# Three edits to a two-layer attention and recurrence kernel: a norm moved ahead, one pair of products reordered, and a duration changed in the table that orders the work

## The chip, the cores and the metric

The kernel runs on one core of a Trainium2 chip. The metric is the device time of one execution in microseconds (us). Five engines take part: PE (matrix products, with PEld for its weight loads), DVE (vector operations), ACT (activations, copies, casts), POOL (little used here) and SP (which issues the DMAs). Each engine works through its own list of instructions strictly in order and waits on semaphores for the others. All times below come from the profile of one execution of the kernel before, and from its three timed runs.

## The reference

The input is one sequence of 1024 tokens with 1024 features, everything in float32.

- Layer 0: RMS norm, then attention with a sliding window of 128 keys and a learned sink per head (16 query heads, 4 key and value heads of 64, rotary embedding on 16 of the 64 dimensions), an output projection, and the residual sum. Then RMS norm and an MLP `square(relu(h @ w_up)) @ w_down` with 4096 hidden units, and the residual sum.
- Layer 1: RMS norm, then a gated linear recurrence (HGRN2) with 8 heads of 128 by 128 state, in chunks of 64 tokens: `o_intra` needs, for each pair of tokens t >= s of a chunk, `sum_d q[t,d] * exp(b[t,d] - b[s,d]) * k[s,d]`, where `b` is the running sum of the log forget gates; `o_inter` comes from the state. Then a norm, an output gate, a projection and the residual sum. Then the same MLP.
- A final RMS norm.

## The kernel before, in words

**Tiling.** Activations stand transposed: 8 tiles of 128 features by 512 tokens for each half (hf 0 and 1) of the tokens. A product in full precision is made of three passes (`mm3`): each operand is split into a high and a low part, and high by high, high by low and low by high are summed in PSUM. Each pass is one matmul of 128x512. The MLPs and the projections of layer 1 use Strassen-like products: seven products named 1 to 7 in place of eight.

**What sets the order.** Python code first records every operation with its operands (`Schedule.add`), the engines that may do it, and a cost in nanoseconds for each. `Schedule.order` then plays the program through with these costs, engine by engine: whenever an engine is free in this play it takes the ready operation with the best rank. PE operations are ranked by their place in the program, the others by a due time worked back from PE, and `lead` moves an operation's rank ahead by 120 ns for each unit. Buffers of a kind (58 `a`, 20 `t`, 7 `m`, 4 `p` and 4 `q` PSUM banks and so on) are given out in the order of the program, as earlier ones come free in the play. What comes out is one sequence of all operations, which is issued in just that order, and the semaphores are put in by the framework from it: where an instruction stands later in the sequence than another that reads or writes the same buffer, it waits for that one. The costs are therefore not on the chip; they only decide the order.

**The norm of layer 0's second half.** `attention` projects half 0 (`qkv(0)`), loads half 1 of x, scales it by the gain (`scaled`), and then interleaves `attend(0)` with `qkv(1)`, and `attend(1)` with `o_proj(0)`. The norm itself is one number per token, `token_rstd(sum_squares(...))`: eight squares on ACT, seven sums on DVE, four narrow matmuls into a PSUM bank of kind `q`, then a chain of six small operations on DVE with a square root on ACT between the first and the second. It is applied when a projection leaves PSUM. `scaled` returns it as a function, and `qkv(1)` calls that at its first step, which comes after the first piece of `attend(0)`.

**The MLP's first products.** `pair(m)` (m = 0 to 15) works out hidden tiles m and m+16 by the seven products; 1, 6, 7 and 4 add up in one bank, `main`, and are read out between (u1, u2, u3, and at the end relu and square); 5 and 3 add up in `side`, 2 has a bank `own`. Each product is 12 matmuls. Behind the last pair, `down` starts: it needs the four `q` banks as its own `main` and the four `p` banks as `side`.

**The recurrence.** For each of the 8 heads (e) the score matrix of a chunk is built in six levels (lg 0 to 5): `products` makes a batch of 16 narrow matmuls (8 for each half, in alternating halves of the PE columns, so 64x32 outputs, or 64x64 for the diagonal), and `merge` on DVE copies the wanted elements into `scores` under a mask. Levels 1 and 2 share one PSUM bank, and so do levels 3 and 4: 16 matmuls of `first` go to `low`, 16 of `second` to `high`, then `merge(low)` and `merge(high)`. Before each level `double` updates q and k on DVE, and `copied` makes copies on ACT. Between the batches PE works on the projections of later heads (`two`), and at the end on `hgrn_out`. The line of `products` that the change touches gives PE's cost of each narrow matmul: `mm` turns its rate into `n * rate / 2.4 + 3` nanoseconds, so 30 for a 64x32 and 58 for a 64x64.

Nearly all rows of the profile name line 372, where every operation is issued, so tiles and shapes tell them apart: `q<-t,t 128*64 128x32` is a narrow product (each is recorded as two matmuls), `q<-a,wh 128*128 128x512` a pass of a wide one, DVE's `COPY_PREDICATED t<-c,q` a merge.

Of the kernel before, what the change touches and what calls it, by code (L numbers as in the profile page):

```python
# [25 lines left out]
MT = FF // P  # L26
# [9 lines left out]
BPH = NBLK // NH  # L36
# [6 lines left out]
CH = 64  # L43
# [93 lines left out]
LEAD = 100  # L137
# [181 lines left out]
class Net:  # L319
# [323 lines left out]
    def pair(self, m, x):  # L643

        w = self.strassen_weights(*(self.io["up"][self.layer, i] for i in (m, m + MT // 2)))

        def read(ps):
            z = self.t()
            self.take(z, ps)
            return z  # L650

        main, side, own = self.psum("q"), self.psum("q"), self.psum()
        self.product(main, w[1], x[1], True)
        u1 = read(main)
        self.product(own, w[2], x[2], True)
        self.product(side, w[5], x[5], True)
        p5 = read(side)
        self.product(main, w[6], x[6], False)
        u2 = read(main)
        self.product(side, w[3], x[3], False)  # L660
        self.product(main, w[7], x[7], False)
        u3 = read(main)
        self.product(main, w[4], x[4], False)
        def kept(name, z):
            self.hid[name, m] = self.keep(z)

        self.add_bank(u1, own)
        h00 = self.square_relu(u1)
        kept(1, h00)
        self.add_bank(u2, side)  # L670
        h01, t5, t6, t4 = self.square_relu(u2), *(self.t() for _ in range(3))
        self.tt("any", t5, h01, h00, ALU.subtract)
        kept(5, t5)
        self.tt("any", p5, p5, u3, ALU.add)
        h11 = self.square_relu(p5)
        kept(3, h11)
        self.tt("any", t6, h11, t5, ALU.subtract)
        kept(6, t6)
        self.tt("any", h01, h11, h01, ALU.subtract)
        kept(7, h01)  # L680
        h10 = self.square_relu(main, True)
        kept(2, h10)
        self.tt("any", t4, h10, t6, ALU.subtract)
        kept(4, t4)
# [374 lines left out]
    def attention(self, layer):  # L1059
        self.v, self.dv, self.ks, self.kl = [], [], [None] * 3, [None] * 3  # L1060
        self.q = [[None] * 2 for _ in range(NBLK)]
        out = [{}, {}]
        self.load_x([0])
        h = [self.scaled(layer, 0)]
        self.attention_constants()
        run(self.qkv(0, *h[0]))
        self.load_x([1])
        h.append(self.scaled(layer, 1))
        interleave(self.attend(0, out[0]), self.qkv(1, *h[1]), 16, 24)
        interleave(self.attend(1, out[1]), self.o_proj(0, out[0]), 24, 8)  # L1070
        self.mlp_first(layer)
        run(self.o_proj(1, out[1]))
# [172 lines left out]
    def recurrence(self, e, ready, totals, out):  # L1245
# [3 lines left out]
        chunk = lambda z, j: z[:, j * CH : j * CH + CH]  # L1249
# [7 lines left out]
        def moved(lg):  # L1257
            return [(k, [parts(chunk(q, j), lg)[:, :, 1] for j in range(2 * BPH)]) for q, f, k, g in gates]
# [10 lines left out]
        def products(part, operands, late, width=CH // 2):  # L1269
            part = part.rearrange("p (c t) -> p c t", c=NC)  # L1270
            for hf, (k, qs) in enumerate(operands):
                for c in range(BPH):
                    for b in range(2):
                        rows = slice(b * CH, b * CH + CH)
                        j = 2 * c + b
                        self.mm(part[rows, hf * BPH + c], chunk(k, j), qs[j], True, True, width, 2.06, "columns", late)

        def merge(part, lg):
            H = 1 << lg
# [6 lines left out]
        def views(operands):  # L1286
            return [z for k, qs in operands for z in (k, *qs)]
# [8 lines left out]
        gates = decayed  # L1296
        late = views(plain) + views(moved(0))
        products(whole, plain, late, CH)
        products(half, moved(0), late)
        mask = self.diag.unsqueeze(1).to_broadcast([P, NC, CH])  # L1300
        self.tt("DVE", scores, whole.rearrange("p (c t) -> p c t", c=NC), mask, ALU.mult)
        merge(half, 0)
        yield
        for lg in range(1, LEVELS, 2):
# [5 lines left out]
            if lg < LEVELS - 1:  # L1310
                second = moved(lg + 1)
                late = views(first) + views(second)
                products(low, first, late)
                products(high, second, late)
                merge(low, lg)
                merge(high, lg + 1)
            else:
                late = views(first) + [z for q, f, k, g in gates for z in (q, k)]
                products(low, first, late)
                cross = self.psum("q")[:CH].rearrange("p (c t) -> p c t", c=NC)  # L1320
                for hf, (q, f, k, g) in enumerate(gates):
                    for c in range(BPH):
                        self.mm(cross[:, hf * BPH + c], chunk(k, 2 * c), chunk(q, 2 * c + 1), True, True, CH, 3.9, "columns", late)
                merge(low, lg)
                weights = []
                for hf in range(NH):
                    s, c = self.t(F32, (P, BPH, 2, CH)), slice(hf * BPH, hf * BPH + BPH)
                    self.memset(s[CH:, :, 0].only(0), 0.0, "Pool")
                    self.copy(s[:CH, :, 0].only(1), scores[:CH, c], 4 * CH)
                    self.copy(s[CH:, :, 1].only(2), scores[CH:, c], 4 * CH)  # L1330
                    self.copy(s[:CH, :, 1].only(3), cross[:, c], 4 * CH)
                    weights.append(s)
                at, tot = self.double(CH, gates, tot, tots, at)
# [149 lines left out]
def run(pieces):  # L1483
    for _ in pieces:
        pass


def interleave(main, other, n_main, n_other):
    done = 0
    for k, _ in enumerate(main):  # L1490
        while done * n_main < (k + 1) * n_other and next(other, run) is not run:
            done += 1
    run(other)
# [81 lines left out]
```

## Time and profile before

| what | value |
|---|---|
| median of 3 runs | 2010.9 us (2010.59 to 2011.6) |
| the profiled execution | 2007.87 us, its span 2005.5 us |
| PE busy | 1979.5 us, 99% of the span, granted clock 0.998 |
| DVE, ACT, POOL busy | 1699.2, 1013.7, 62.7 us |
| chain that ended last | PE 85%, DVE 7%, DMA 3%, issue 2%, ACT 2% |
| 64x32 narrow products | 1536 records (768 products), 51.0 us busy |
| layer 1's recurrence | about 1010 to 1335 us from the span's start |

The span runs from the first to the last instruction; the profiled execution's own time is 2.4 us longer, and 3.0 us below the median of the runs. PE is busy almost throughout, so a list of the places where PE waits says more here than the shares of busy time: `idle before` in a group's row, or a number in square brackets behind a row of the timeline, is PE's idle time ahead of that instruction, and the arrow names what ended it. In the timeline the first column is the start from the beginning of the span, the second the duration of the merged rows; matmuls are pipelined, so the starts that follow each other tell what one costs.

### The profile page before, as it was taken

Reading aid. Unit: us, or ns where it says so; the run is one execution under the profiler, and the core shown is the slowest. Engines: PE = TensorE matmul, PEld = TensorE weight load, DVE = VectorE, ACT = ScalarE, POOL = GpSimd, SP = SyncE. Lnnn points to the kernel's source line nnn. Section 1 sums busy time; section 2 is a strip of 40 time slices with the busy share of each in tenths; the row PEclk is TensorE's granted clock in tenths of the full one; section 3 lists DMA queues with packets and bytes.
Section 4 is the critical chain, followed back from the end, with each engine's and each line's share of the span. In section 5 each row is a group of like instructions: output and inputs, shape, how many; then the busy total and the mean of one; then the engine's idle time right before and its main releaser. Section 6 shows DMA issues by size and latency. Waiting matters only on the chain.

```text
span 2005.5 us, 32701 instructions
## 1 busy us (share of the span) xinstructions
PE 1979.5 (99%) x11404; PEld 1718.5 (86%) x11404; DVE 1699.2 (85%) x3360; ACT 1013.7 (51%) x2045; POOL 62.7 (3%) x124
## 2 busy tenths in 40 slices
PE   9999999999999999999999999999999999999998
PEld 8877788888888888888888888888888888888887
DVE  8999899777778878799898999989977777887787
ACT  6567796554454323255345555554654445323352
POOL 4030100000000000000000000000000000000001
PEclk9999999999999999999999999999999999999999
DMA  6212463544468967745422212667444446886752
GB/s 216 90 53 59 127 222 120 184 167 160 146 204 292 314 217 264 235 163 176 146 63 78 78 59 90 207 208 244 142 167 160 146 162 237 286 301 215 236 179 85
DMA packets 196677, 345.88 MB, mean 172 GB/s; under 512 B 21536, under 2 KB 31776, under 8 KB 196512
## 3 DMA queue, kind: packets, MB, share of 16 engines
q1 hardware_dynamic: 195936, 343.28, 52.0%
q8 instruction: 89, 1.46, 0.3%
q14 instruction: 76, 0.62, 0.1%
q10 hardware_dynamic: 576, 0.52, 0.1%
HBM read 250.39 MB, written 93.32 MB: 171 GB/s over the span
## 4 chain that ended last, share of the span: by engine, by line
PE 85%; DVE 7%; DMA 3%; issue 2%; ACT 2%; POOL 0%; SPq 0%; POOLq 0%; DVEq 0%; ACTq 0%
PE q L372 51%; PE p L372 34%; DVE t L372 3%; DVE a L372 2%; DVE wl L372 1%; ACT t L372 1%; ACT a L372 1%; DMA wr<-in_down 1%; DVE m L372 0%; DMA a<-in_x 0%; ACT wh L372 0%; ACT m L372 0%; DMA t<-d 0%; DMA wr<-in_wqkv 0%; DMA wr<-in_wv 0%
## 5 line engine op out<-in xcount | busy, mean ns | idle before, releaser
L372 PE MATMUL q<-a,wh 128*128 128x512 f32 x2560 | 761.8, 379 | 3.5 <-ACT t L372 3.5
L372 PE MATMUL p<-a,wh 128*128 128x512 f32 x2112 | 644.6, 383 | 0.1
L372 PEld LDWEIGHTS q<-a,wh 128*128 128x128 f32 x2560 | 482.3, 189 | 74.1 <-ACT t L372 5.0
L372 PE MATMUL q<-a,wl 128*128 128x512 f32 x1280 | 484.9, 379 | 0.0
L372 PEld LDWEIGHTS p<-a,wh 128*128 128x128 f32 x2112 | 394.2, 189 | 54.6 <-issue 1.2
L372 PE MATMUL p<-a,wl 128*128 128x512 f32 x1056 | 401.6, 381 | 0.0
L372 ACT CAST a<-t 128x512 fp32r<-128x512 f32 x283 | 172.0, 619 | 286.0 <-PE q L372 142.8
L372 PEld LDWEIGHTS q<-a,wl 128*128 128x128 f32 x1280 | 241.9, 189 | 34.3
L372 ACT ACTIVATE t<-t 128x512 f32<-128x512 f32 x272 | 171.1, 631 | 189.8 <-DVE t L372 182.2
L372 DVE TENSOR_TENSOR wl<-wr,wh 128x512 fp32r<-128x512 f32 x352 | 240.6, 686 | 11.7 <-ACT wh L372 3.9
L372 DVE TENSOR_TENSOR t<-t,t 128x512 f32<-128x512 f32 (+3 forms) x364 | 224.9, 638 | 26.8 <-ACT t L372 23.1
L372 PEld LDWEIGHTS p<-a,wl 128*128 128x128 f32 x1056 | 199.7, 189 | 26.8 <-issue 0.4
L372 DVE TENSOR_TENSOR a<-t,a 128x512 fp32r<-128x512 f32 (+1 forms) x326 | 217.2, 685 | 6.4 <-ACT a L372 6.0
L372 DVE TENSOR_TENSOR wl<-m,wh 128x512 fp32r<-128x512 f32 x248 | 170.5, 689 | 16.7 <-ACT wh L372 10.1
L372 ACT COPY t<-q 128x512 f32<-128x512 f32 (+2 forms) x214 | 119.4, 560 | 112.6 <-PE q L372 111.5
L372 ACT CAST wh<-wr 128x512 fp32r<-128x512 f32 x173 | 106.5, 618 | 100.2 <-PE p L372 45.7
L372 DVE TENSOR_TENSOR m<-wr,wr 128x512 f32<-128x512 f32 x160 | 110.0, 689 | 39.7 <-DMA wr<-in_down 24.0
L372 DVE CAST wh<-wr 128x512 fp32r<-128x512 f32 x179 | 76.5, 427 | 78.9 <-PE q L372 47.2
L372 ACT CAST wh<-m 128x512 fp32r<-128x512 f32 x154 | 94.8, 618 | 57.2 <-PE q L372 35.1
L372 PE MATMUL p<-wh,a 128*128 128x512 f32 x352 | 110.9, 385 | 0.0
L372 PEld LDWEIGHTS q<-t,t 128*64 128x64 f32 (+1 forms) x2160 | 95.2, 144 | 14.0 <-issue 5.3
L372 PE MATMUL q<-t,t 128*64 128x32 f32 (+2 forms) x2160 | 104.1, 229 | 1.8 <-DVE t L372 1.3
(130 smaller groups left out, 2056.8 us busy)
## 6 DMA issues: line engine op xcount, KB each, us to landing
d<-t SPq DMA_DIRECT2D x276, 256.0 KB, 2.8
t<-d SPq DMA_DIRECT2D x264, 256.0 KB, 4.5
wr<-in_down SPq DMA_DIRECT2D x256, 256.0 KB, 3.9
wr<-in_up SPq DMA_DIRECT2D x128, 256.0 KB, 2.9
a<-d SPq DMA_DIRECT2D x60, 256.0 KB, 5.1
wr<-in_wqkv SPq DMA_DIRECT2D x48, 256.0 KB, 3.0
d<-a SPq DMA_DIRECT2D x48, 256.0 KB, 3.5
wr<-in_win SPq DMA_DIRECT2D x48, 256.0 KB, 2.9
```

The source lines that it names most:

```text
L372: fn(*[place(a) for a in args], **{k: place(v) for k, v in kw.items()})
```

## The change

Three edits:

1. `attention`: behind `scaled(layer, 1)` the norm of the second half is worked out at once, ahead of `attend(0)`, with a lead of 200. `qkv(1)` then gets the finished value.
2. `pair`: the seven products of the last pair (m = 15, in both MLPs) come in the order 1, 5, 6, 2, 7, 3, 4; those of the others stay at 1, 2, 5, 6, 3, 7, 4. What is read out between them and all that follows is the same.
3. `products` in the recurrence: the rate that gives a narrow matmul's cost is 3.6 where the output is 32 wide and 2.4 where it is 64 wide, in place of 2.06 for both. By the formula above that is 51 and 67 ns in place of 30 and 58.

No operation is added or left out, on any engine.

```diff
--- before.py
+++ after.py
@@ -650,17 +650,14 @@
         main, side, own = self.psum("q"), self.psum("q"), self.psum()
-        self.product(main, w[1], x[1], True)
-        u1 = read(main)
-        self.product(own, w[2], x[2], True)
-        self.product(side, w[5], x[5], True)
-        p5 = read(side)
-        self.product(main, w[6], x[6], False)
-        u2 = read(main)
-        self.product(side, w[3], x[3], False)
-        self.product(main, w[7], x[7], False)
-        u3 = read(main)
-        self.product(main, w[4], x[4], False)
+        got = {}
+        for name in (1, 5, 6, 2, 7, 3, 4) if m == MT // 2 - 1 else (1, 2, 5, 6, 3, 7, 4):
+            ps = main if name in (1, 6, 7, 4) else own if name == 2 else side
+            self.product(ps, w[name], x[name], name in (1, 2, 5))
+            if name in (1, 5, 6, 7):
+                got[name] = read(ps)
+        u1, p5, u2, u3 = (got[name] for name in (1, 5, 6, 7))
...
@@ -1066,6 +1063,10 @@
         h.append(self.scaled(layer, 1))
+        self.s.lead = 2 * LEAD
+        r = h[1][1]()
+        self.s.lead = 0
+        h[1] = h[1][0], lambda: r
         interleave(self.attend(0, out[0]), self.qkv(1, *h[1]), 16, 24)
...
@@ -1273,7 +1274,7 @@
-                        self.mm(part[rows, hf * BPH + c], chunk(k, j), qs[j], True, True, width, 2.06, "columns", late)
+                        self.mm(part[rows, hf * BPH + c], chunk(k, j), qs[j], True, True, width, 3.6 if width < CH else 2.4, "columns", late)
```

The edits change the issued order in four places only: around 55 to 100 us, 590 to 650 us and 1670 to 1750 us of the profile before, and over the recurrence. Everywhere else each engine's list is the same. The names in the rows below are a buffer's kind and its number; behind the underscore stands a number of the framework's own.

**PE in the recurrence, head 2, levels 1 and 2.** `q3081` is the shared bank; the first four rows of each list are the 16 products of `low`, the others those of `high` (t3076 and t3036 are q and k of half 0, t3077 and t3037 those of half 1). What an instruction waits for stands in brackets. Before:

```order
L372 MATMUL q3081_12369<-t3078_12349,t3079_12337 64x32 [waits Activation_49]
L372 MATMUL q3081_12369<-t3078_12349,t3079_12337 64x32 x7
L372 MATMUL q3081_12369<-t3078_12349,t3080_12343 64x32 [waits Activation_49]
L372 MATMUL q3081_12369<-t3078_12349,t3080_12343 64x32 x7
L372 MATMUL q3081_12369<-t3076_12235,t3036_12222 64x32 [waits DVE_49]
L372 MATMUL q3081_12369<-t3076_12235,t3036_12222 64x32 x7
L372 MATMUL q3081_12369<-t3077_12246,t3037_12230 64x32 [waits DVE_49]
L372 MATMUL q3081_12369<-t3077_12246,t3037_12230 64x32 x7
```

With the change:

```order
L372 MATMUL q3081_12369<-t3078_12352,t3079_12340 64x32 [waits Activation_49]
L372 MATMUL q3081_12369<-t3078_12352,t3079_12340 64x32 x7
L372 MATMUL q3081_12369<-t3078_12352,t3080_12345 64x32 [waits Activation_49]
L372 MATMUL q3081_12369<-t3078_12352,t3080_12345 64x32 x7
L372 MATMUL q3081_12369<-t3076_12235,t3036_12222 64x32 [waits DVE_49]
L372 MATMUL q3081_12369<-t3076_12235,t3036_12222 64x32 x7
L372 MATMUL q3081_12369<-t3077_12246,t3037_12230 64x32 [waits DVE_49]
L372 MATMUL q3081_12369<-t3077_12246,t3037_12230 64x32
L372 MATMUL q3081_12369<-t3077_12246,t3037_12230 64x32 [waits DVE_49]
L372 MATMUL q3081_12369<-t3077_12246,t3037_12230 64x32 x5
```

The last eight products of `high` now have a second wait for DVE in their midst, since `merge(low)`, which reads this bank, stands in the sequence behind the second of them and ahead of the third. Of the 16 shared banks (8 heads, two each) two have such a place in the kernel before, head 1's levels 1 and 2 and head 6's levels 3 and 4; with the change all 16 have one, behind 20 to 29 of the bank's 32 products. Around the batches one to three wide matmuls change sides.

**PE at the end of layer 0's last pair.** `q1706` is `main`, `q1707` is `side`, `q1727` and `q1728` are the first two banks of `down`; wh1702/wl1703 are the weights of product 7, wh1700/wl1701 those of 3, wh1704/wl1705 those of 4. Before, from the last matmul of product 7 to the first of product 4:

```order
L372 MATMUL q1706_6780<-a979_4114,wl1703_6861 128x512
L372 MATMUL q1727_7003<-a1739_6827,wh1736_6909 128x512 [waits PE_49]
L372 MATMUL q1727_7003<-a1740_6841,wh1736_6909 128x512
L372 MATMUL q1727_7003<-a1739_6827,wl1737_6919 128x512 [waits DVE_49]
L372 MATMUL q1728_7013<-a1739_6827,wh1736_6909 128x512 [waits PE_49]
L372 MATMUL q1728_7013<-a1740_6841,wh1736_6909 128x512
L372 MATMUL q1728_7013<-a1739_6827,wl1737_6919 128x512
L372 MATMUL q1706_6780<-a982_4120,wh1704_6876 128x512 [waits Activation_49]
```

With the change, from the same matmul on:

```order
L372 MATMUL q1706_6780<-a979_4114,wl1703_6861 128x512
L372 MATMUL q1707_6839<-a954_3890,wh1700_6822 128x512
L372 MATMUL q1707_6839<-a955_4168,wh1700_6822 128x512
L372 MATMUL q1707_6839<-a954_3890,wl1701_6834 128x512
L372 MATMUL q1707_6839<-a957_3953,wh1700_6822 128x512
L372 MATMUL q1707_6839<-a958_4173,wh1700_6822 128x512
L372 MATMUL q1707_6839<-a957_3953,wl1701_6834 128x512
```

All 12 matmuls of product 3 now stand between product 7 and product 4; the six of `down` come behind product 4. Layer 1's last pair moves in the same way.

**ACT at the norm's square root.** sm267 (before) and sm239 (with the change) hold the norm; an `ACT_TABLE_LOAD` stands ahead of the root. Before:

```order
L372 COPY m243_372<-q244_1106 128x2x128 [waits PE_49]
L372 COPY m243_372<-q245_1116 128x2x128 [waits PE_49]
L372 ACT_TABLE_LOAD
L372 ACTIVATE sm267_1143<-sm266_1137 128x4 [waits DVE_49]
L372 COPY m272_375<-q273_1132 128x2x128 [waits PE_49]
```

With the change:

```order
L372 ACTIVATE t236_916<-a212_570 128x512 [waits DVE_49,Activation_49]
L372 ACT_TABLE_LOAD
L372 ACTIVATE sm239_1005<-sm238_998 128x4 [waits DVE_49]
L372 CAST wh296_1008<-wr295_910 128x512 [waits DMAHW2_49,PE_49,Activation_49]
L372 ACTIVATE a242_1017<-q241_1000 64x512 [waits PE_49]
```

Before, the root stands in the midst of the first attention blocks' copies; with the change it stands directly behind the last of the eight squares, ahead of the first transposed queries. On PE the norm's four narrow matmuls move in the same way, to the end of half 0's projection, and the `q` bank they use is asked for ahead of those of `attend(0)`.

## The prediction

> **What bounds the kernel now.** I read the page's busy times and its chain first.
>
> ```profile
> span 2005.5 us, 32701 instructions
> PE 1979.5 (99%) x11404; PEld 1718.5 (86%) x11404; DVE 1699.2 (85%) x3360; ACT 1013.7 (51%) x2045; POOL 62.7 (3%) x124
> PE 85%; DVE 7%; DMA 3%; issue 2%; ACT 2%; POOL 0%; SPq 0%; POOLq 0%; DVEq 0%; ACTq 0%
> ```
>
> PE is busy 99% of the span and carries 85% of the chain. No edit adds or removes a matmul, so the time moves only by the places where PE stands still: whatever PE waits more or less is the change, and any saving on DVE, ACT or the queues is worth what it takes from a PE wait. All waits of PE together are the 26 us between 2005.5 and 1979.5. So I went on to the list of waits, here for the recurrence (1040 to 1340 us: total, times, longest).
>
> ```profile
> PE q L372 <- DVE t L372: 1.3, 2, 0.8
> PE q L372 <- DMA t<-v: 0.4, 1, 0.4
> PE q L372 <- DVE a L372: 0.3, 1, 0.3
> PE q L372 <- DVE m L372: 0.2, 1, 0.2
> ```
>
> In 300 us PE waits 2.2 us, and 1.3 of them are two waits for DVE. A better order can win at most the other 0.9 us here. The two waits are what the third edit is about, so I looked them up in the timeline. First a shared bank without one (head 0, levels 1 and 2; all rows are PE, then the merge on DVE):
>
> ```profile
> 1021.23 2.06 PE L372 MATMUL q<-t,t 128*64 128x32 f32 x64
> 1023.22 0.48 PE L372 MATMUL p<-a,wh 128*128 128x512 f32 x1
> ...
> 1023.33 0.74 DVE L372 COPY_PREDICATED t<-c,q 128x256 f32<-128x256 int32 x1 [0.57 <-PE q L372]
> ```
>
> The 32 products (64 records) take 1.99 us to the start of the next wide matmul, and the merge begins behind the last of them. Now the two with a wait, head 1's levels 1 and 2, and head 6's levels 3 and 4:
>
> ```profile
> 1063.04 1.93 PE L372 MATMUL q<-t,t 128*64 128x32 f32 x58
> 1065.79 0.42 PE L372 MATMUL q<-t,t 128*64 128x32 f32 x6 [0.82 <-DVE t L372]
> 1066.14 0.48 PE L372 MATMUL p<-a,wh 128*128 128x512 f32 x1
> ...
> 1065.01 0.72 DVE L372 COPY_PREDICATED t<-c,q 128x256 f32<-128x256 int32 x1 [0.36 <-PE q L372]
> ...
> 1280.09 1.71 PE L372 MATMUL q<-t,t 128*64 128x32 f32 x52
> 1282.33 0.54 PE L372 MATMUL q<-t,t 128*64 128x32 f32 x12 [0.53 <-DVE t L372]
> 1282.80 0.48 PE L372 MATMUL p<-a,wh 128*128 128x512 f32 x1
> ...
> 1281.85 0.43 DVE L372 COPY_PREDICATED t<-c,q 128x256 f32<-128x256 int32 x1 [0.80 <-PE q L372]
> ```
>
> PE stops behind 58 records (29 products) and behind 52 (26 products). DVE was idle, waiting for PE, and then ran the merge of `low`; it ends at 1065.73 and 1282.28, and PE goes on 0.06 and 0.05 us later. These are exactly the two banks whose merge stands in the midst of `high` in the order of before. The batches take 1066.14 - 1063.04 = 3.10 us and 2.71 us: **1.11 and 0.72 us more** than the 1.99 of the unbroken one.
>
> **The corrected durations (third edit).** With them the order has such a place in all 16 shared banks. A merge there waits for the product just ahead of it, and the product behind it waits for the merge; PE takes its list in order, so nothing covers the gap. That is the merge's own duration and the way there and back, wherever in the bank it falls. The two old ones stay. New are seven on levels 1 and 2 and seven on levels 3 and 4: 7 x 1.11 + 7 x 0.72 = 7.8 + 5.0 = **+12.8 us**. I see nothing that excludes a part of it, so this is a lower bound for the term.
>
> Above it lies DVE's own lateness. In both stops seen DVE stood waiting, so they hold none. With the change up to four other operations of DVE stand between the last operand and the merge. The stretches differ (us, then PE, PEld, DVE):
>
> ```profile
> 1050.00:1090.00 40.00, 39.18 (x405) 34.61 (x404) 34.73 (x76) 18.41 (x37) 2.42 (x3) 1.00 0.26 85
> 1090.00:1130.00 40.00, 39.89 (x402) 34.77 (x401) 38.16 (x91) 25.89 (x51) 0.56 (x2) 1.00 0.21 67
> ...
> L372 DVE TENSOR_TENSOR wl<-wr,wh 128x512 fp32r<-128x512 f32 x352 | 240.6, 686 | 11.7 <-ACT wh L372 3.9
> ```
>
> Where the stop of 1065 us was measured DVE is busy 87% of the time, in the next stretch 95%. If one operation of 0.69 us were still ahead of each of the 16 merges, that is 11.0 us; the lower end is nothing. PE itself falls behind by the stops, which gives DVE time, so I stay near the rows seen and take three of 16: **+2.1**. What the better durations win is bounded by the 0.9 us of other waits, and PE arriving later helps them too: **-0.5** (0 to -0.9). That batches start up to three wide matmuls (0.65 us) earlier I put at nothing: no PE wait above is for ACT's copies, which end ahead of them.
>
> **The last pair (second edit).** PE, then ACT:
>
> ```profile
> 605.02 0.59 PE L372 MATMUL q<-a,wh 128*128 128x512 f32 x2
> 605.45 0.38 PE L372 MATMUL q<-a,wl 128*128 128x512 f32 x1
> 607.09 0.70 PE L372 MATMUL q<-a,wh 128*128 128x512 f32 x2 [1.26 <-ACT t L372]
> ...
> 604.76 1.29 ACT L372 ACTIVATE t<-t 128x512 f32<-128x512 f32 x2 [1.34 <-DVE t L372]
> 605.96 0.60 ACT L372 CAST wh<-m 128x512 fp32r<-128x512 f32 x1
> 606.47 0.58 ACT L372 COPY t<-q 128x512 f32<-128x512 f32 x1
> ...
> 1694.56 0.38 PE L372 MATMUL q<-a,wl 128*128 128x512 f32 x1
> 1697.19 0.70 PE L372 MATMUL q<-a,wh 128*128 128x512 f32 x2 [2.25 <-ACT t L372]
> ```
>
> Two wide matmuls take 0.43 us (605.02 to 605.45), one 0.22. PE loses 607.09 - 605.45 - 0.22 = 1.42 us, and 2.41 at the other layer, 3.83 in all, because product 4 waits for the copy of u3 out of `main`, and ACT does that copy behind a relu that waited for DVE. With product 3 between them, 12 x 0.22 = 2.6 us of matmuls cover that copy, and ACT's relu ahead of it belongs to a product that ended 2.6 us sooner. Late next is `down`'s fourth bank: it is `main` itself and needs ACT's relu of product 4, with only nine matmuls (2.0 us) ahead of it and another relu and square (1.29) in ACT's list before. I take **-3.5**, from -3.8 (all of it) to -1.8 (1 us lost again at each).
>
> **The norm (first edit).** ACT, then PE:
>
> ```profile
> 73.13 0.62 ACT L372 CAST wh<-wr 128x512 fp32r<-128x512 f32 x1 [5.51 <-PE q L372]
> 84.79 1.28 ACT L372 ACT_TABLE_LOAD   x1
> 86.49 0.20 ACT L372 ACTIVATE sm<-sm 128x4 f32<-128x4 f32 x1 [0.41 <-DVE sm L372]
> 87.82 1.28 ACT L372 ACT_TABLE_LOAD   x1
> 89.11 0.40 ACT L372 ACTIVATE m<-m,sm 128x129 f32<-128x129 f32 x1
> ...
> 78.95 0.63 PE L372 MATMUL q<-c,a 128*128 128x128 f32 x4 [0.66 <-DVE a L372]
> 82.72 0.46 PE L372 MATMUL q<-a,a 128*128 128x256 f32 x2 [0.55 <-DVE a L372]
> 84.20 0.95 PE L372 MATMUL q<-c,t 128*128 128x1 f32 x8
> 91.85 0.63 PE L372 MATMUL q<-c,m 128*128 128x128 f32 x4 [0.73 <-ACT m L372]
> ```
>
> PE's 0.95 us at 84.20 only moves. On ACT the table load of 1.28 us and a wait of 0.41 leave the softmax of the first blocks, on which PE waits 0.73 us at 91.85, and go into 5.51 us of idle time before 73.13. Against that six small operations on DVE (put at the root's 0.20 each, 1.2 us) come ahead of the transposed queries, for which PE waits 0.66 and 0.55 us, and the norm takes the first free `q` bank, so that each transpose gets the next. Ends: -1.9 if all three waits go, +1.2 if DVE's work is all added. I take **-0.4**: 0.7 won at 91.85, 0.3 lost at the transposes, a quarter of the bound, since DVE's list has the last of their sums earlier.
>
> The trace shows a load as 1.28 us, and the exponential starts 0.01 us behind it. The Trainium skill (ScalarE: Activation LUTs, What ACT_TABLE_LOAD costs) has the same 1283 ns, but adds a drain of about 1380 for each switch; no row here shows it. By that figure ACT would be freed of 2.7 us, all three waits could go, and this term, as an estimate from that page, would be -1.9 and the sum +9.0.
>
> **The sum:** 12.8 + 2.1 - 0.5 - 3.5 - 0.4 = **+10.5 us** on the profiled execution's 2007.87, so 2018.4. The runs shown have their median 3.0 us above that execution; against them it is 2010.9 + 10.5 = **2021.4 us**.
>
> **Rivals.**
>
> *The waits cost nothing, and the kernel is faster.* If the second wait inside a bank were met before PE arrives, because it stood for an operand rather than for the merge, the sum would be -3.5 - 0.4 - 0.5 = -4.4: 2006.5 us. For it: only two stops have been seen. Against it: both end with the merge, to 0.06 us, and the merge begins only when PE has stopped. It decides from the point where a merge is over before PE has finished the product ahead of the wait. 0.07. The Trainium skill speaks against it too (PSUM — Partial Sum Buffer, PSUM bank collisions raise a hardware error): two engines must not touch one bank at once, so the merge's read and PE's writes have to be kept apart; no run here shows what happens otherwise.
>
> *DVE is late at most of the stops:* 11.0 in place of 2.1, +19.4, 2030.3 us. For it: 95% busy in stretches, and list places behind four operations. Against: DVE waited for PE at both stops seen. 0.12.
>
> *The last pair wins nothing,* since `down` waits for its fourth bank as long as product 4 did for u3: +3.5, 2024.9 us. For it: ACT has two relu and square pairs in that place. Against: `down` has nine matmuls to do first. 0.08.
>
> **How the numbers follow.** 0.73 for the forecast, 0.12, 0.08 and 0.07 for the rivals. The low end takes the bounds 12.8 - 0.9 - 3.8 - 1.9 = +6.2, a little below which I go: 2016. The high end takes half of DVE's upper bound and the poor ends of both others, 12.8 + 5.5 - 1.8 + 1.2 = +17.7: 2028. Outside are the first two rivals, 0.19. What the measurement can tell from no change is 0.2%, 4 us. All cases but the first rival are slower by more (0.93), and from them and it I move 0.03 to the middle, for a floor that turns out much lower or waits that cost half: slower 0.91, within 0.2% 0.03, faster 0.06.
>
> **What would show it.** PE's group of 64x32 products should have some 11 us of idle time before it, released by `DVE t` (7 x 0.82 + 7 x 0.53 = 9.5 more; the rest of the 12.8 lies in modelled ends), and each of the 16 banks should fall into two pieces with a merge between, released by PE. If DVE is late, the merges show no wait for PE and the gaps exceed 0.82 and 0.53. The waits `ACT t` before product 4 should be gone, and `ACT m` at 91.85. I am wrong if the batches of 32 products still take 1.99 us.

## The result, and the profile after

| | before | with the change |
|---|---|---|
| median | 2010.74 us (4 runs, 2005.92 to 2011.6) | 2032.18 us (4 runs, 2028.2 to 2035.23) |
| profiled execution, its span | 2007.87, 2005.5 | 2035.23, 2033.1 |
| granted clock, mean | 0.998 | 0.993 |

The change makes the kernel slower: ratio **1.011**, 95% interval 1.0086 to 1.0135, +21.4 us of medians. Predicted were +10.5 us and at most 2028.

The page's span, busy times and chain of the kernel with the change:

```profile
span 2033.1 us, 32709 instructions
PE 1993.8 (98%) x11404; PEld 1725.6 (85%) x11404; DVE 1705.3 (84%) x3366; ACT 1010.6 (50%) x2039; POOL 60.9 (3%) x124
PE 72%; DVE 15%; DMA 6%; ACT 3%; issue 3%; SPq 0%; POOL 0%; DVEq 0%; POOLq 0%; ACTq 0%
```

PE does the same 11404 matmuls, but is busy for 14.3 us more, and the span is 27.6 us longer. So there are two losses: some 13 us in which PE stands, and 14 us in which it seems to work longer at the same work. DVE's share of the chain has gone from 7 to 15%. Where PE stands says the list of its waits, here from 1000 to 1400 us (total, times, longest), and the group of the 64x32 products (idle time behind the bar):

```profile
PE q L372 <- DVE t L372: 15.7, 16, 2.0
```

```profile
L372 PE MATMUL q<-t,t 128*64 128x32 f32 x1536 | 54.7, 224 | 15.9 <-DVE t L372 15.7 <-ACT t L372 0.2
```

The two waits of before, 1.3 us, have become 16 with 15.7 us, one for each shared bank (some 11 were forecast for this row), and the group is busy for 54.7 us in place of 51.0, which we put down to the modelled ends of batches that now come in two pieces. The timeline has the lengths. These are second pieces: head 0 (levels 1 and 2, then 3 and 4), and levels 1 and 2 of heads 2, 3, 4 and 6:

```profile
1023.82 0.89 PE L372 MATMUL q<-t,t 128*64 128x32 f32 x24 [0.83 <-DVE t L372]
1031.51 0.43 PE L372 MATMUL q<-t,t 128*64 128x32 f32 x8 [0.53 <-DVE t L372]
...
1113.66 0.54 PE L372 MATMUL q<-t,t 128*64 128x32 f32 x12 [1.68 <-DVE t L372]
...
1159.50 0.85 PE L372 MATMUL q<-t,t 128*64 128x32 f32 x10 [1.99 <-DVE t L372]
...
1208.50 0.54 PE L372 MATMUL q<-t,t 128*64 128x32 f32 x12 [1.70 <-DVE t L372]
...
1300.87 0.65 PE L372 MATMUL q<-t,t 128*64 128x32 f32 x14 [1.67 <-DVE t L372]
```

Levels 3 and 4 cost what they cost before, 0.53, at every head. Levels 1 and 2 have 0.83 at head 0, but up to 1.99 at the others. The reason stands in DVE's list. PE and DVE around head 2's bank:

```profile
1110.27 1.71 PE L372 MATMUL q<-t,t 128*64 128x32 f32 x52
1110.92 0.73 DVE L372 COPY_PREDICATED t<-c,q 128x256 f32<-128x256 int32 x1
1111.44 0.73 DVE L372 TENSOR_TENSOR wl<-wr,wh 128x512 fp32r<-128x512 f32 x1
...
1112.28 0.69 DVE L372 TENSOR_TENSOR m<-m,wr 128x512 f32<-128x512 f32 x1
1112.89 0.72 DVE L372 COPY_PREDICATED t<-c,q 128x256 f32<-128x256 int32 x1
...
1114.47 0.63 PE L372 MATMUL p<-a,wl 128*128 128x512 f32 x1
1114.89 1.06 PE L372 MATMUL p<-a,wh 128*128 128x512 f32 x2
```

PE's first piece is over at 1111.98. DVE has no idle time, and only at 1112.89 does it come to the merge of level 1: ahead of it in its list are the level 0 merge (the first `COPY_PREDICATED`) and operations on weights for wide matmuls, two of them of 0.7 us. PE waits until all of that is done. The last rows show the other loss. The wide matmuls behind the stop come every 0.42 us (1114.47 to 1114.89), where they come every 0.22 elsewhere. That is the clock. Stretches around the stop (us, then PE, PEld, DVE, ACT, POOL busy, granted clock, DMA share, GB/s):

```profile
1111.01:1114.42 3.41, 1.73 (x47) 1.57 (x44) 3.41 (x10) 0.36 (x1) 0.56 (x2) 1.00 0.29 77
1114.43:1117.84 3.41, 3.41 (x9) 2.69 (x8) 2.82 (x9) 1.23 (x3) 0.00 (x0) 0.50 0.31 81
...
1158.79:1162.20 3.41, 2.70 (x15) 2.28 (x16) 2.67 (x8) 1.54 (x3) 0.00 (x0) 0.50 0.26 77
```

From 1114.43 on the clock is granted at half for 3.41 us, and PE counts as busy throughout (the last row, at head 3, is used below). In short stretches one sees each fall:

```profile
1114.40:1114.60 0.20, 0.20 (x2) 0.16 (x2) 0.20 (x2) 0.00 (x0) 0.00 (x0) 0.56 0.14 51
1158.70:1158.90 0.20, 0.00 (x0) 0.00 (x0) 0.20 (x2) 0.00 (x0) 0.00 (x0) 0.74 0.44 61
1209.90:1210.10 0.20, 0.20 (x2) 0.17 (x2) 0.20 (x2) 0.20 (x2) 0.00 (x0) 0.74 0.19 31
1254.30:1254.50 0.20, 0.20 (x3) 0.17 (x2) 0.20 (x2) 0.10 (x1) 0.00 (x0) 0.68 0.00 0
1302.10:1302.30 0.20, 0.20 (x3) 0.14 (x2) 0.20 (x2) 0.20 (x2) 0.00 (x0) 0.65 0.93 297
...
1165.50:1165.70 0.20, 0.20 (x2) 0.14 (x1) 0.20 (x2) 0.00 (x0) 0.00 (x0) 0.69 0.00 0
```

A mean of 0.56 over 0.20 us is 0.176 us at half, so the clock fell at 1114.42; the others, worked out in the same way, came at 1158.80, 1210.00, 1254.37 and 1302.16, in or just behind the level 1 and 2 stops of heads 2 to 6. The distances are 44.4, 51.2, 44.4 and 47.8 us: 13, 15, 13 and 14 times 3.413. The clock is set on a fixed grid of 3.413 us. Head 3's stretch has double length (the last row, to 1165.6), the others one step: 4 x 3.41 + 6.8 = 20.5 us at half clock. Of these PE works all but 0.7 us (2.70 of 3.41 at head 3), so about 19.8 / 2 = **9.9 us** are lost.

The sum of the third edit in this execution: 12.8 us for the way from product to merge and back, as predicted, plus DVE's lateness (the eight waits on levels 1 and 2 have 15.7 - 8 x 0.53 = 11.5 us, and 8 x 0.82 = 6.6 is their bare price, so 4.9), plus 9.9 at half clock: 27.6. The second edit gives 2.9 back, the first 0.2 (both below): 24.5, between the medians' +21.4 and this execution's own +27.4.

### The profile page after: what moved, and what is told of

Read it like the earlier page. It is cut to its first block, busy times and chain, and to the rows that moved or that the text cites. A ratio compares the mean times of both kernels' runs of the same rounds, so it can differ in the third digit from the quotient of the medians.

```text
span 2033.1 us, 32709 instructions
## 1 busy us (share of the span) xinstructions
PE 1993.8 (98%) x11404; PEld 1725.6 (85%) x11404; DVE 1705.3 (84%) x3366; ACT 1010.6 (50%) x2039; POOL 60.9 (3%) x124
## 4 chain that ended last, share of the span: by engine, by line
PE 72%; DVE 15%; DMA 6%; ACT 3%; issue 3%; SPq 0%; POOL 0%; DVEq 0%; POOLq 0%; ACTq 0%
PE q L372 45%; PE p L372 27%; DVE t L372 7%; DVE a L372 3%; DVE wl L372 3%; DMA t<-d 2%; ACT t L372 2%; DVE m L372 1%; DMA wr<-in_down 1%; DMA wr<-in_wv 1%; ACT a L372 1%; ACT wh L372 1%; DMA a<-in_x 0%; SPq L372 0%; DMA wr<-in_up 0%
## 5 line engine op out<-in xcount | busy, mean ns | idle before, releaser
L372 PEld LDWEIGHTS p<-a,wh 128*128 128x128 f32 x2112 | 398.9, 191 | 56.8 <-issue 1.2
L372 PE MATMUL p<-a,wl 128*128 128x512 f32 x1056 | 406.3, 385 | 0.0
L372 PE MATMUL q<-t,t 128*64 128x32 f32 (+2 forms) x2160 | 108.3, 230 | 16.7 <-DVE t L372 15.7
```

Of the source, the lines that this page charges most:

```text
L372: fn(*[place(a) for a in args], **{k: place(v) for k, v in kw.items()})
```

## The experiments

Theory A: the third edit is the whole loss, 16 stops of PE and the half clock that the longest of them bring. B: the other edits cost something too. C: the new order has a price of its own, beside the stops. All ratios are to the kernel before on the same chip, with 95% intervals.

### The edits apart

**The third edit alone.** On the kernel before:

```diff
-  self.mm(part[rows, hf * BPH + c], ..., width, 2.06, "columns", late)
+  self.mm(part[rows, hf * BPH + c], ..., width, 3.6 if width < CH else 2.4, "columns", late)
```

> The third edit alone on the kernel before: durations 3.6 and 2.4 in place of 2.06. Theory A (the loss is all in the third edit: 16 stops of PE inside the shared banks, some 17 us more than the two of before, and about 9.5 us in which the wide matmuls behind the longest stops come at half the granted clock): +22 to +28 us, near 2036, all 16 banks with a stop, clock of 0.9 over the 20 us stretches around the stops of heads 2 to 6. Theory B (the two other edits cost something too, and the third only the 12 to 15 us that was predicted): +12 to +16 us, near 2025.

Measured: 2032.1 us against 2007.85, ratio 1.0123 (1.0108 to 1.0138), +24.3 us, inside the +22 to +28 of theory A. Its group of 64x32 products and one of its 20 us stretches:

```profile
L372 PE MATMUL q<-t,t 128*64 128x32 f32 x1536 | 54.3, 223 | 14.9 <-DVE t L372 14.9
```

```profile
1060.00:1080.00 20.00, 18.08 (x237) 15.25 (x236) 17.49 (x39) 9.14 (x17) 0.61 (x2) 0.91 0.16 54
```

At head 1's stop (1060 to 1080 us) the mean clock is 0.91, a step at half, which the execution above did not have there.

**The first and second edit together,** the rate back at 2.06.

> The first and second edit with the old durations. Theory A: the two stops before product 4 (1.42 and 2.41 us) and the wait of 0.73 us at the softmax are gone, nothing else moves: -3 to -5 us, near 2007, the granted clock 1.00 over the whole recurrence, two banks with a stop as before. Theory B: +6 us or more, about 2017.

Measured: 2005.49 us against 2007.85, ratio 0.9987 (0.9978 to 0.9997), -2.4 us (-4.4 to -0.6). B falls; of the -3 to -5 us that theory A gave, the middle of the interval has a little less.

**The second edit alone.** The loop of the change's `pair`, nothing else.

> The second edit alone on the kernel before. As predicted: the two stops before product 4 go, -3.5 us (-3.8 to -1.8), a ratio near 0.998. Rival: down's fourth bank takes the wait over, 0 us, ratio 1.000.

Measured: 2003.77 us against 2006.67, ratio 0.9985 (0.9976 to 0.9994), -2.9 us. As predicted; the rival falls.

**The first edit alone.** The four lines of the change's `attention`.

> The first edit alone on the kernel before. As predicted: -0.4 us (-1.9 to +1.2), a ratio of 0.9991 to 1.0006, which the measurement can not tell from no change; the wait of 0.73 us at the first softmax gone. Rival by the page on activation tables: -1.9 us, 0.9990.

Measured: 2006.21 us against 2007.62, ratio 0.9998 (0.9989 to 1.0007). No change that can be told; -1.9 us, which the Trainium skill would give (ScalarE: Activation LUTs, What ACT_TABLE_LOAD costs; a drain of about 1380 ns beside each load), lies inside the interval of -2.2 to +1.4 as well.

**Only the rate of the 64 wide products** (the first two edits, and this):

```diff
-  width, 3.6 if width < CH else 2.4, ...
+  width, 2.06 if width < CH else 2.4, ...
```

> The first two edits and of the third only the rate of the 64 wide products (2.4; the 32 wide stay at 2.06). In the order two banks have a merge in their midst (both of head 6), 14 have none. Theory A (the count of such places decides): the ratio of the first two edits alone, 0.997 to 1.000, clock 1.00. Rival C (any change of these durations worsens the order): 1.004 or more.

Measured: 2005.88 us against 2007.62, ratio 0.9996 (0.9986 to 1.0006). So it is the rate of the 32 wide products that brings the stops: in the order (not run on the chip) 3.6 for these alone gives 15 banks with a merge in their midst.

### The stops taken away

**The merge of low behind the whole bank.** `high` is an extra operand for the order alone; the instruction is the same:

```diff
-  merge(low, lg)
+  merge(low, lg, [high])      # in merge: ins = [mask, part, *behind]
```

> All three edits, but merge(low) also reads high, so that it stands behind all 32 products of the bank in the order; the merge itself is the same. Theory A: no stop inside a bank, so neither the 17 us of stops nor the 9.5 us at half clock: the changed durations cost nothing by themselves, and with the other two edits and without the two stops of before it is 2010.7 - 4 - 1.7 = about 2005 us, granted clock 1.00 in the recurrence. Rival C (the new order is worse for other reasons, DVE's late merges or other buffers): still 8 us or more above before, 2019 or higher.

Measured: 2006.22 us against 2007.85, ratio 0.9996 (0.9987 to 1.0005). PE's longest waits from 1040 to 1340 us:

```profile
PE q L372 <- DMA t<-v: 2.0, 3, 0.9
PE q L372 <- ACT t L372: 1.0, 2, 0.7
```

The stops are gone, the clock is 1.00, and with them the loss. The -5.7 us that were expected are not all there, though: new waits of 2.0 us for the DMA of `v` and 1.0 for ACT stand in the recurrence, 0.2 for that DMA and none for ACT with the old rates (next experiment). So C has some 3 us in it, where the merge is held back and the rates are new. What makes that DMA late was not tried.

**The kernel before with that edit alone.**

> The kernel before with nothing but merge(low) behind all 32 products of its bank. Theory A: its two stops of 0.82 and 0.53 us go, -1.7 us, 2009 us, which the measurement can hardly tell from no change. Rival C: the merges of all the other banks stood there already, so nothing else can move; if it comes out 4 us or more slower, keeping the merge back has a price of its own.

Measured: 2004.84 us against 2007.85, ratio 0.9986 (0.9977 to 0.9996), -3.0 us (-4.6 to -0.8), which holds the 1.7 that the two old stops were expected to cost. PE's wait for the DMA of `v` from 1000 to 1360 us is 0.2 us here.

**The same order, without the merges.** All three edits, each operation at its place in the order, but the low merges are not put on the chip:

```diff
-  merge(low, lg)
+  merge(low, lg, False)   # recorded with its cost, issues nothing
```

> All three edits, every engine's list the same as with the change, but the merges of low (levels 1 and 3) are not done on the chip, so the scores lack these levels. Theory A (stops and half clock are all of the loss, and both hang on these 16 instructions): no stop inside a bank, clock 1.00 in the recurrence, and the ratio to before at that of the first two edits, 0.997 to 1.000. Rival C (the new order has a price of its own, beside the stops): the ratio stays above 1.002.

Measured: 2003.4 us against 2007.62, ratio 0.9977 (0.9968 to 0.9987). The group of 64x32 products, and the stretch from 1000 to 1360 us:

```profile
L372 PE MATMUL q<-t,t 128*64 128x32 f32 x1536 | 50.5, 223 | 0.1
```

```profile
1000.00:1360.00 360.00, 358.37 (x3451) 313.53 (x3450) 324.37 (x749) 196.99 (x388) 8.06 (x18) 1.00 0.36 117
```

This settles where the loss is. With every other instruction in the order of the change, 0.1 us of waits ahead of the narrow products and the clock at 1.00 over the recurrence, the kernel is as fast as its first two edits make it. The 16 instructions make 1.0110 - 0.9977 = 0.0133, 27 us (21 to 32); the terms above give 12.8 + 4.9 + 9.9 and 1.8 for the two stops of before, 29. C falls for the order of the change itself. Leaving the 16 merges out also frees DVE of some 9 us of work, which this run can't tell from the stops; the run above that holds the merges back, but does them all, is 1.0110 - 0.9996 below the change, 23 us, without that help.

### The length of the stops, and the clock

**The level 0 merge left out.** It stands just ahead of the merge of level 1 in DVE's list; again recorded, not issued:

```diff
+  if not lg:
+      self.s.add({"DVE": (lambda: None, 70 + NC * CH // 2 * 1.04)}, [target], [mask, part])
+      return
```

> All three edits and the same order of every engine, but the level 0 merge (0.70 us of DVE, the work just ahead of the level 1 merge in the list of DVE) is left out on the chip, so the scores lack level 0's elements. The merges that stop PE are all there. Theory A (the seven or so level 1/2 stops over 1.1 us are long because DVE comes 0.3 to 1.2 us late to the merge, and a 3.41 us stretch of a fixed grid in which PE does little but wait and narrow products is followed by one at half clock): the stops of heads 1 to 6 fall from 1.45-2.2 us to 1.0-1.5 us, 4 us in all, and five or six stretches at half clock go or become one or two, another 6 to 9 us: 2032 - 11 = about 2021, near what was predicted for the change. Rival D (the stops' length is the way from merge to PE, not DVE's lateness): the stops stay at 1.45-2.2 us, and the time within 3 us of 2032. Rival E (the half clock comes with any stop in a bank, whatever its length): stops shorter, the half clock stays: 2028.

Measured: 2024.54 us against 2006.67, ratio 1.0091 (1.0072 to 1.0109), 4 us better than the change by the middle of intervals that overlap, where 11 were expected. The four executions fall in two pairs: 2020.55 and 2021.73 us at a mean clock of 0.997, 2027.35 and 2029.91 at 0.994. A clock lower by 0.003 over 2027 us is some 6 us, most of the 7.5 between the pairs, so the expected 2021 was reached where the clock fell less often; the profile is of the last, 2029.91. Second pieces on levels 1 and 2 of heads 2, 3 and 4:

```profile
1114.65 0.54 PE L372 MATMUL q<-t,t 128*64 128x32 f32 x12 [1.12 <-DVE t L372]
1160.58 0.64 PE L372 MATMUL q<-t,t 128*64 128x32 f32 x8 [1.74 <-DVE t L372]
1209.07 0.54 PE L372 MATMUL q<-t,t 128*64 128x32 f32 x12 [1.14 <-DVE t L372]
```

The waits went from 1.68 to 1.12, 1.99 to 1.74 and 1.70 to 1.14. The stops do hang on what DVE has ahead of the merge, so D falls. The level 0 merge, 0.7 us long, holds DVE's list for 0.52 us from its start to the next one's (1110.92 to 1111.44 in the change), so at heads 2 and 4 all of it is won, and at head 3 half. What is left above 0.82 is the other operations ahead, and the clock still falls behind three stops (heads 1 to 3). Head 2's bank again:

```profile
1112.18:1115.59 3.41, 2.29 (x61) 2.11 (x59) 3.41 (x12) 0.72 (x2) 0.56 (x2) 1.00 0.29 80
1115.60:1119.01 3.41, 3.41 (x10) 2.70 (x9) 2.64 (x8) 1.58 (x3) 0.00 (x0) 0.50 0.28 78
```

Here 1.12 us of PE's standing still in a step of 3.41 were enough. Head 4, with 1.14, kept the full clock (the step behind this one is at 1.00), so the length of a stop does not decide alone:

```profile
1207.76:1211.17 3.41, 2.27 (x26) 1.93 (x23) 3.41 (x11) 1.14 (x2) 0.27 (x2) 1.00 0.36 102
```

PE is busy for as long as at head 2, but 1.6 us of it are wide matmuls (from 1209.54 on) and at head 2 only 0.5 (from 1115.12 on). Rival E already fails on the profile of the change: 16 banks have a stop there, and only five falls follow.

**Narrow products without a stop.** The kernel of "the merge of low behind the whole bank", with the products of each shared bank done twice:

```diff
   products(low, first, late)
   products(high, second, late)
+  products(low, first, late)
+  products(high, second, late)
```

> The kernel without stops (2006 us), but all 32 products of each shared bank are done twice, 64 narrow products without a pause: 16 x 2.0 = 32 us more of PE, 2038 us. It asks whether narrow products count as activity for the clock. Theory N1 (they count about half of a wide matmul): no stretch at half clock, although PE does nothing but narrow products for 4.0 us: 2038 or a little less, since DVE gets time. Theory N2 (they count as nothing, so that a batch and the stop add up): a stretch of 3.4 us at half clock behind most of the 16 banks, and about 1.6 us lost in each, up to 25 us more, 2055 to 2063.

Measured, one run: 2033.85 us, 27.6 more than without the repetition. Its clock is 1.00 in the recurrence. The steps of the grid are found by counting back from the fall of the clock at the run's end (0.74 over 0.40 us: 2023.79). The one from 1112.44 lies wholly inside head 2's batch of 3.93 us:

```profile
1112.27 3.93 PE L372 MATMUL q<-t,t 128*64 128x32 f32 x128
```

```profile
1112.44:1115.85 3.41, 3.41 (x123) 3.41 (x122) 3.41 (x12) 0.88 (x2) 0.47 (x2) 1.00 0.17 49
1115.85:1119.26 3.41, 3.41 (x27) 2.99 (x24) 3.38 (x12) 2.13 (x5) 0.09 (x1) 1.00 0.32 109
2023.60:2024.00 0.40, 0.06 (x1) 0.09 (x1) 0.16 (x1) 0.00 (x0) 0.00 (x0) 0.74 0.00 0
```

A whole step of narrow products alone keeps the clock. N2 falls. The other side is in the kernel before, at the stop of 2.25 us between wide matmuls (layer 1's last pair); its grid is counted back from its own fall at the end (1996.64, from a mean of 0.94 between 1994 and 1997 us):

```profile
1692.87:1696.28 3.41, 2.07 (x10) 1.48 (x8) 2.71 (x6) 2.07 (x5) 0.00 (x0) 1.00 0.73 252
1696.28:1699.69 3.41, 2.50 (x12) 2.21 (x13) 3.41 (x6) 3.27 (x7) 0.00 (x0) 1.00 0.95 337
```

PE stands still for 1.34 of 3.41 us, longer than in the step of 1112.18 above (1.12), and the clock stays; the rest is wide work. So neither a stop nor narrow work alone brought the half clock, but both in one step of the grid.

No merge is needed for it. The run without the low merges has one such fall, in layer 0, where PE stops for 1.13 us ahead of a norm's narrow matmuls (8 records, one column each); 1.4 of the 2.28 us that PE is busy in the step ahead are wide:

```profile
316.34 1.05 PE L372 MATMUL q<-c,t 128*128 128x1 f32 x8 [1.13 <-DVE t L372]
```

```profile
314.99:318.40 3.41, 2.28 (x15) 1.95 (x14) 3.41 (x7) 3.17 (x7) 0.00 (x0) 1.00 0.15 55
318.40:321.81 3.41, 3.41 (x9) 2.70 (x8) 3.31 (x6) 2.45 (x5) 0.00 (x0) 0.50 0.07 16
```

**Wide work put into the bank.** All three edits, and:

```diff
   products(low, first, late)
+  for q, f, k, g in gates:
+      self.mm(high, self.ident, q[:, : NC * CH // 2], True, True, NC * CH // 2, 4)
   products(high, second, late)
```

> All three edits, and between the products of low and of high two extra matmuls of 128x256 in full float32 into high's half (their result is overwritten): work of 2 x 0.43 us on the full array in each of the 16 banks, 13.8 us more for PE. The merge of low now stands ahead of the first or second product of high, so PE still stops once in each bank, but 0.86 us later after low's end. Theory A (the clock goes by how much PE does in a fixed 3.41 us, wide work counting most): no stretch at half clock (-9.5 us), and the stops shorten by up to what is added (-0.7 to -0.86 each, -12 us): useless work costs nothing, 2022 to 2028 us against 2032, a ratio of 1.006 to 1.010. Rival E (any stop in a bank brings the half clock, or it is the merge's collision with PE's bank): the half clock stays, ratio 1.011 or more. Rival F (the extra work adds up with the stops): ratio 1.014 and more.

Measured: 2043.33 us against 2007.62, ratio 1.0185 (1.0169 to 1.0201). The whole recurrence as one stretch, and from the timeline PE and the merge of level 1 at head 2's bank:

```profile
1000.00:1380.00 380.00, 362.80 (x3426) 309.03 (x3425) 320.50 (x738) 185.80 (x366) 7.75 (x18) 1.00 0.30 96
```

```profile
1113.76 0.70 PE L372 MATMUL q<-t,c 128*128 128x256 f32 x2 [0.54 <-DVE t L372]
...
1114.39 1.13 PE L372 MATMUL q<-t,t 128*64 128x32 f32 x32
...
1115.45 0.70 PE L372 MATMUL q<-t,c 128*128 128x256 f32 x2
1116.18 0.72 DVE L372 COPY_PREDICATED t<-c,q 128x256 f32<-128x256 int32 x1 [0.19 <-PE q L372]
1116.96 1.12 PE L372 MATMUL q<-t,t 128*64 128x32 f32 x32 [0.81 <-DVE m L372]
```

For the clock the outcome is A's, and E falls: PE still stops in the banks, and the clock is 1.00 over all of it. That wide work counts for more this run does not show by itself, since the poorest step of its grid has PE busy for 2.38 us, above the 1.7 to 2.3 ahead of the falls. For the time rival F holds: one extra product went ahead of `low` and waits itself (0.54), and the merge of level 1 waits for the other (0.19 of idle time, released by PE, at 1116.18), although it reads only `low`. DVE's lateness is gone from this stop (0.81 in place of 1.68), but its bare price stays: it begins when PE has reached the merge's place in the order, wherever that is. And the extra matmuls are dearer than expected, 0.63 us each (1113.76 to 1114.39), some 20 us in all and not 13.8.

### A version that beats both

The first two edits, the old rate, and the merge of low behind the whole bank.

> The first and second edit, the old durations, and merge(low) behind all 32 products of its bank: the parts that were faster one by one (-2.4 and -3.0 us). If they add up: -5 us, a ratio of 0.997 to 0.998, below both kernels. If they do not, since the order around the recurrence differs once more: -2 us or nothing.

Measured: 2002.53 us against 2006.67, ratio 0.9978 (0.9969 to 0.9987), -4.1 us. The gains add up, and this is faster than the kernel before and than the kernel with the change.

## Why the prediction was right, and where it was wrong

**What bounds the kernel: right in part, and here is the step that failed by most.** The prediction has "the time moves only by the places where PE stands still". PE's time is the kernel's time, and its waits carried some two thirds of the difference (12.8 + 4.9 of 27.6 us). The other 9.9 us are the same matmuls taking longer at half clock, for which the prediction has no term.

**The third edit, the price of a stop: right.** All 16 banks stop PE. The bare price is 0.82 and 0.53 us, as read from two stops of before (0.83 at head 0, 0.53 at all of levels 3 and 4), so the 12.8 us stand. That they were "a lower bound" was right too.

**The third edit, DVE's lateness: mis-sized.** The step that failed here is "I stay near the rows seen and take three of 16: +2.1". The runs showed 4.9. The ground given, that PE's falling behind gives DVE time, does not hold on levels 1 and 2 of the later heads: at head 2, shown above, DVE works without a pause up to the merge, on weights among other things. The rows of before that showed DVE idle at a stop were of two banks only, and the list with the change, which had been read, has other work ahead. Heads 2, 3, 4 and 6 were late by more than one operation of 0.69 us (0.85 to 1.17), so the bound of one operation each did not hold for a single stop, though 11.0 held for the sum.

**The third edit, a term that is missing: the clock, 9.9 us.** The prediction's rows of before show the granted clock at 1.00, and it takes no other into account. This carried most of the miss. With 4.9 in place of 2.1 and 9.9 added the sum is 10.5 + 2.8 + 9.9 = +23.2, against the medians' +21.4 (17 to 27). The rival "DVE is late at most of the stops", 2030.3, came nearest by its figure, but for the wrong reason: it has 11.0 us of lateness and no clock. The two others fell: the waits were not met before PE arrived, and the last pair did win.

**The gain of the better durations: wrong in kind.** There was none to see: -0.5 was taken, and with the stops gone the new rates cost some 3 us in one form (the ratio 0.9996 against 0.9978, merge of low held back in both) and nothing in the other (0.9977 without the merges).

**The last pair: right.** -3.5 forecast, -2.9 measured alone (-4.8 to -1.2). In the profile of the change, PE at the first matmuls of product 4 and of the fourth bank of `down`:

```profile
604.28 0.70 PE L372 MATMUL q<-a,wh 128*128 128x512 f32 x2
...
609.33 0.70 PE L372 MATMUL q<-a,wh 128*128 128x512 f32 x2 [0.25 <-ACT t L372]
```

The wait of 1.26 is gone; late next is the fourth bank of `down`, as said, with 0.25 and not 1 us. At layer 1 no wait is left.

**The norm: right in size, wrong in its step.** PE's waits from 60 to 100 us with the change (before: 1.2 for `DVE a` and 0.7 for `ACT m`):

```profile
PE q L372 <- DVE a L372: 1.0, 2, 0.7
PE q L372 <- DVE m L372: 0.7, 2, 0.4
```

The wait for ACT at 91.85 is gone, as foreseen, and two others for DVE of 0.7 us in all stand in its place: 0.2 us won. The transposes lost nothing, so that the size came out near is chance. The drain of some 1380 ns that the Trainium skill has (ScalarE: Activation LUTs, What ACT_TABLE_LOAD costs) is not seen here either: the exponential starts 0.02 us behind its load.

```profile
86.44 1.28 ACT L372 ACT_TABLE_LOAD   x1
87.74 0.41 ACT L372 ACTIVATE m<-m,sm 128x129 f32<-128x129 f32 x1
```

**The chances.** The sign was given 0.91 and is right. The range ended at 2028 because it took half of one unknown cost; a term nobody had thought of is not in such a bound.

## What to carry to other kernels

Where a list of one engine is cut by a wait for another, price the cut by what the other engine has ahead in its own list at that point, not by the cuts that happened to find it idle. Correcting a planner's costs need not help: the order came out such that a read lay in the midst of writes to the same bank, which the planner holds to be independent and the waits in the program do not; telling the planner of that dependence (one extra operand) repaired it. And when PE stops next to narrow matmuls, look at the granted clock behind the stop, since the wide matmuls there can cost twice.

## What the runs showed of the hardware

A stop of 1.1 to 2.0 us in the midst of a batch of narrow products could cost 1.7 us and more behind it, by the clock: 3.41 us of work at half speed, 1.7 lost, and twice that at head 3, where the step at half clock was itself poor in work. The step ahead of the two falls shown inside a bank had PE busy for 1.73 us of 3.41 (change) or 2.29 (level 0 left out), mostly with narrow products; 2.07 us of wide work kept the clock, and so did 2.27 us that were mostly wide and 3.41 us of narrow work. How the two are weighed against each other the runs do not fix. Since the grid does not follow the program, the same stop falls into one step or two: head 1's brought half clock with the third edit alone (1.40 us) and not in the profile of the change (1.42 us).

The Trainium skill (TensorE: Matmul & The Clock Gate, What's actually happening) has a free-running window of 3413 ns and a half rate behind it, and the trace agrees (steps of 3.413 us, wide matmuls every 0.42 in place of 0.22). Its advice for avoiding drops in mid-kernel (same page, Why this matters for your kernels) is no idle gap above about 3 us; by it no stop here, with 1.99 us the longest in a bank, would have cost any clock. The measurement differs: 1.12 us was enough where the rest of the window held narrow products.
